# Where the FFN's moving operands lie in SBUF: one remainder of 512 bytes, or six

## The chip, the cores and the metric

One core of a Trainium2 chip runs the whole program. The metric is device time in microseconds, the median of several runs; before the change it is 2765.83 us, of three runs between 2764.89 and 2770.86.

## The reference

One decoder block on a sequence of 256 positions and 2048 channels in float32. A conditioning vector gives shifts, scales and gates. Two token mixers (Mamba-2 and Gated DeltaNet) run side by side on the normalised input and are merged. What the change touches is the dense FFN behind them:

```
x = x + gate_m * mix
h = modulate(rms_norm(x, norm_ffn_w), shift_f, scale_f)
gate, up = split(h @ w_gate_up)              # 2048 -> 2 x 5632
x = x + gate_f * ((silu(gate) * up) @ w_down) # 5632 -> 2048
return rms_norm(x, final_norm_w)
```

## The kernel before, in words

Activations lie transposed: a tile has 128 channels as partitions and, for each of KT = 16 (or FT = 44 in the FFN's hidden layer) groups of 128 channels, a row of S = 256 float32, one per position. A row is 1024 bytes, so all rows of a tile start at the same remainder modulo 512 bytes.

Every linear layer is a list of items. An item is one 512 KB block of weights: eight matrices of 128 x 128. `load_next` (L136) queues its DMA on SP, ACT copies it to `hi` with reduced precision (L146), DVE makes the rest `lo = raw - hi` (L148), and `lin_items` (L209) or `quad_items` (L230) issue three matmuls for each matrix:

```
T_.matmul(ps[:, t, :], hi[:, s], h_, ...)           # L221: stationary hi, moving high part
T_.matmul(ps[:, t, :], hi[:, s], al[:, kt, :], ...) # L222: stationary hi, moving low part
T_.matmul(ps[:, t, :], lo[:, s], h_, ...)           # L223: stationary lo, moving high part
```

The second argument is the stationary operand (the weights, 512 bytes per partition, at a multiple of 512), the third the moving operand (one row of the activation tile). So an item is 24 matmuls of 128x128 by 128x256, each with its weight load. `pump` (L155) issues one item at a time and keeps up to four prepared ahead; it also calls the posts, the work behind a finished accumulation. The order of the work on every engine is the order of these calls.

The FFN begins at L1252. A pool `ff` opens at the address where the mixer's pools were; a pad of OFF = 48 words comes first, so that the four tiles h2h, h2l (KT rows each, high and low part of h) and fh, fl (FT rows each, of the hidden layer) start 192 bytes past a multiple of 512. The mixer's moving operands (hh, hl, yh, yl, mh, ml) start at the same remainder in this program. L1266 to L1270 write the rows of h2h and h2l while the first items already run. The gate-up product is 24 items by `quad_items` (six accumulators side by side, so that four rows of h feed six items) and 152 by `lin_items`, in which the even items use rows 0 to 7 of h and the odd ones rows 8 to 15. `ffn_post` (L1222) writes row j of fh and fl. The down product is 88 items: for each of 8 pairs of output tiles, the 44 rows of fh and fl twice in order.

The z items (`z_items`, L255) have the operands the other way round: a row block of hh or hl is stationary and 512 columns of the weight tile, which start at a multiple of 512 bytes, are moving.

Of the kernel before, what the change touches and what calls it, by code (L numbers as in the profile page):

```python
# [10 lines left out]
F32 = mybir.dt.float32  # L11
F32R = mybir.dt.float32r
# [7 lines left out]
P = 128  # L20
D = 2048
S = 256
KT = D // P
# [3 lines left out]
FT = 44  # L27
# [23 lines left out]
NCA = 2  # L51
LZ = 2

OFF = 48

VB_ADA = 0
VN_MIX = 96
# [11 lines left out]
C_NSL = 2  # L69
C_LV = 6  # L70
C_I16 = C_LV * P + 3 * 64


@with_exitstack
def block_kernel(ctx: ExitStack, tc: tile.TileContext, xT, cvec, vec, dskip, consts,
# [44 lines left out]
    def vcol(i):  # L120
        return vs[:, i:i + 1]
# [33 lines left out]
    def pump():  # L155
        while items and len(ready) < LA + 1:
            load_next()
        while dots:
            dots.popleft()()
        did, old = False, len(posts)  # L160
        if ready and ready[0][2] <= st_["done"]:
            mm, post, need, sync, hi, lo = ready.popleft()
            if sync:
                finish_posts()
            old = len(posts)
            mm(hi, lo)
            posts.extend(post)
            st_["mm"] += 1
            did = True
        for _ in range(min(old, 1)):  # L170
            posts.popleft()()
        st_["wait"] -= 1.0
        if st_["gen"] is None and gens and gens[0][1] <= st_["mm"]:
            finish_posts()
            st_["gen"] = gens.popleft()
            st_["wait"] = 0.0
        if st_["gen"] is not None and (st_["wait"] <= 0.0 or not did):
            try:
                st_["wait"] = max(st_["wait"], -0.99) + next(st_["gen"][0]) * st_["gen"][2]
            except StopIteration:  # L180
                st_["gen"] = None
                st_["done"] += 1
        if old == 0 and len(posts) > 1:
            posts.popleft()()
        while len(posts) > PQ:
            posts.popleft()()
        st_["pumped"] += 1
        if side and st_["side"] and st_["pumped"] % st_["side"] == 0:
            side.popleft()()

    def flush():
        while items or ready or gens or st_["gen"] is not None:
            pump()
        finish_posts()
# [14 lines left out]
    def lin_items(blocks, xh, xl, nk, done, need=0, sync=False, late_need=0):  # L209
        hold = {}  # L210
        def mk(bi):
            def mm(hi, lo):
                ah, al = (xh(), xl()) if callable(xh) else (xh, xl)
                if bi == 0:
                    hold["ps"] = plin.tile([P, 2, S], F32, tag="lin", name="ps_lin")
                ps = hold["ps"]
                for j in range(BLK):
                    t, kt = divmod(bi * BLK + j, nk)
                    s = slice(j * P, (j + 1) * P)
                    h_ = ah[kt // 8][:, kt % 8, :] if isinstance(ah, list) else ah[:, kt, :]  # L220
                    T_.matmul(ps[:, t, :], hi[:, s], h_, start=kt == 0, stop=False)  # L221
                    T_.matmul(ps[:, t, :], hi[:, s], al[:, kt, :], start=False, stop=False)  # L222
                    T_.matmul(ps[:, t, :], lo[:, s], h_, start=False, stop=kt == nk - 1)  # L223
            return mm
        for bi, src in enumerate(blocks):
            last = bi == len(blocks) - 1
            post = [lambda f=f: f(hold["ps"]) for f in done] if last else []
            add_item(src, mk(bi), post, late_need if last and late_need else need, sync and bi == 0)
# [82 lines left out]
    def sq_finish():  # L311
        ps = bank("ps_sq", (P, S))
        for i, k in enumerate("ab"):
            for t in range(2):
                T_.matmul(ps, ones, sqa[k][:, t, :], start=i + t == 0, stop=i + t == 2)
        return ps

    def rstd_T(pool, ps):
        r = pool.tile([P, S], F32, tag="rstd", name="rstd")
        A.activation(r, ps, AF.Sqrt, scale=1.0 / D, bias=EPS)  # L320
        V.reciprocal(r, r)
        return r
# [18 lines left out]
    def finish_side():  # L341
        while side:
            side.popleft()()
        while dots:
            dots.popleft()()

    def ada_fin(j0, j1):
        V.tensor_tensor(ada[:, j0:j1], ada2[:, j0:j1, 0], ada2[:, j0:j1, 1], ADD)
        V.tensor_tensor(ada[:, j0:j1], ada[:, j0:j1], vs[:, VB_ADA + j0:VB_ADA + j1], ADD)
# [7 lines left out]
    with tc.tile_pool(name="st", bufs=1) as st:  # L357
# [97 lines left out]
        r = rstd_T(st, ps)  # L455
# [10 lines left out]
        for q in range(1, 4):  # L466
# [9 lines left out]
            if q == 2:  # L476
# [6 lines left out]
                lv = st.tile([P, 3, 64], F32, name="lv")  # L483
                nc.sync.dma_start(lv, consts[:, C_LV * P:C_I16].rearrange("p (a b) -> p a b", b=64))
                V.tensor_copy(lvm, lv)
# [230 lines left out]
    def gdn_mix(hu, units):  # L716
        unit = units[hu]
        nxt = units[hu + 1] if hu + 1 < NHU else None
        if hu == 0:
            pools["gp"] = gs.enter_context(tc.tile_pool(name="gp", bufs=1))  # L720
            pools["gsm"] = gs.enter_context(tc.tile_pool(name="gsm", bufs=2))
            pools["i16"] = pools["gp"].tile([64, 256], F32, name="i16")
            nc.sync.dma_start(pools["i16"], consts[0:64, C_I16:C_I16 + 256])
            seg_in, seg_out, squares, ssq, kq, scales, n_tile, store = gdn_head(hu, unit)
# [474 lines left out]
    def res_post(j, gate, pool):  # L1199
        def f(ps):  # L1200
            x2 = pools["accs"]
            for t in range(2):
                i = 2 * j + t
                V.scalar_tensor_tensor(x2[:, i, :], ps[:, t, :], gate[:, i:i + 1], x2[:, i, :], MUL, ADD)
            sq = pool.tile([P, 2, S], F32, tag="th" if j else "cacc", name="sq", bufs=1 if j or pool is not gl_ else NCA)
            A.activation(sq, x2[:, 2 * j:2 * j + 2, :], AF.Square)
            if j == 0:
                sqa["a"] = sq
            elif j < 7:
                G.tensor_tensor(sqa["a"], sqa["a"], sq, ADD)  # L1210
            else:
                sqa["b"] = sq
        return [f]
# [36 lines left out]
    phase_a.close()  # L1250

    with tc.tile_pool(name="ff", bufs=1) as ff:  # L1252
        ff.tile([P, OFF], F32, name="off")
        h2h = ff.tile([P, KT, S], F32R, name="h2h")
        h2l = ff.tile([P, KT, S], F32R, name="h2l")
        fh = ff.tile([P, FT, S], F32R, name="fh")
        fl = ff.tile([P, FT, S], F32R, name="fl")
        F_.update(h=h2h, l=h2l, fh=fh, fl=fl, ff=ff)
        tmps = {}
        for t in range(KT + 1):  # L1260
            if t in (5, 9, 13):
                for _ in range(6):
                    pump()
            if t < KT:
                tmps[t] = ff.tile([P, S], F32, tag="fth", name="htmp", bufs=2)
                V.scalar_tensor_tensor(tmps[t], x2[:, t, :], wsf[:, t:t + 1], rf, MUL, MUL)  # L1266
                A.activation(h2h[:, t, :], tmps[t], AF.Identity, bias=ada[:, 48 + t:49 + t])
            if t > 0:
                V.scalar_tensor_tensor(h2l[:, t - 1, :], tmps[t - 1], ada[:, 47 + t:48 + t],
                                       h2h[:, t - 1, :].bitcast(F32), ADD, SUB)  # L1270
        while items:
            pump()
        finish_side()
        gf = ff.tile([P, KT], F32, name="gf")
        for j in range(8):
            lin_items([w_dn[j, b] for b in range(11)], fh, fl, FT, res_post(j, gf, ff))
        ada_fin(80, 96)
        V.tensor_scalar(gf, ada[:, 80:96], 0.5, None, MUL)
        while len(items) > 20:
            pump()  # L1280
        for t in (1, 4, 7):
            A.activation(x2[:, t, :], x2[:, t, :], AF.Identity, scale=vcol(VN_FIN + t))
        A.activation(dum, ones[:, 0:1], AF.Sqrt)
        flush()
        r = rstd_T(ff, sq_finish())
        for t in range(KT):
            if t in (1, 4, 7):
                G.tensor_tensor(x2[:, t, :], x2[:, t, :], r, MUL)
            else:
                V.scalar_tensor_tensor(x2[:, t, :], x2[:, t, :], vcol(VN_FIN + t), r, MUL, MUL)  # L1290
            if t % 2 == 1:
                (nc.sync if t % 4 == 1 else nc.scalar).dma_start(out[:, t - 1:t + 1, :], x2[:, t - 1:t + 1, :])
# [101 lines left out]
```

## Time and profile before

| what | value |
|---|---|
| median of the runs | 2765.83 us |
| the profiled execution's own time | 2744.2 us |
| its span, first to last instruction | 2742.4 us |
| TensorE (PE) busy | 2665.7 us, 97% |
| VectorE (DVE) busy | 1884.0 us, 69% |
| ScalarE (ACT) busy | 1371.5 us, 50% |
| mean granted TensorE clock | 0.988 |
| FFN's first and last matmul | 1997.6 us, 2727.2 us |

Matmuls overlap: the duration that the profile gives for one is longer than the distance to the next one's start. What a row of matmuls costs is read from the starts, in the timeline. PEld is the weight load, which runs beside the matmul before it. A granted clock of 1.00 is 2.4 GHz, 0.50 is 1.2 GHz.

### The profile page before, as it was taken

Reading aid. Unit: us, or ns where it says so; the run is one execution under the profiler, and the core shown is the slowest. Engines: PE = TensorE matmul, PEld = TensorE weight load, DVE = VectorE, ACT = ScalarE, POOL = GpSimd, SP = SyncE. Lnnn points to the kernel's source line nnn. Section 1 sums busy time; section 2 is a strip of 40 time slices with the busy share of each in tenths; the row PEclk is TensorE's granted clock in tenths of the full one; section 3 lists DMA queues with packets and bytes.
Section 4 is the critical chain, followed back from the end, with each engine's and each line's share of the span. In section 5 each row is a group of like instructions: output and inputs, shape, how many; then the busy total and the mean of one; then the engine's idle time right before and its main releaser. Section 6 shows DMA issues by size and latency. Waiting matters only on the chain.

```text
span 2742.4 us, 51781 instructions
## 1 busy us (share of the span) xinstructions
PE 2665.7 (97%) x20930; PEld 2547.5 (93%) x20930; DVE 1884.0 (69%) x2794; ACT 1371.5 (50%) x2250; POOL 306.7 (11%) x684
## 2 busy tenths in 40 slices
PE   6999999999999999989999999999999999999998
PEld 5889899999999999988899989999989999999997
DVE  7787767769687786857767667768666666655444
ACT  3325554655546455544666656554444444444442
POOL 0000312303123131210000000002100000000000
PEclk8999999999999999999999999999999999999999
DMA  8886657566575665735545445447756666655553
GB/s 334 299 325 231 208 173 253 182 208 229 168 248 175 227 213 173 253 131 179 190 156 177 167 163 176 162 153 268 241 178 216 228 224 225 228 199 194 192 193 131
DMA packets 183283, 566.90 MB, mean 207 GB/s; under 512 B 34753, under 2 KB 43777, under 8 KB 183041
## 3 DMA queue, kind: packets, MB, share of 16 engines
q1 hardware_dynamic: 154306, 552.56, 59.0%
q10 hardware_dynamic: 28736, 11.01, 1.5%
q8 instruction: 164, 2.69, 0.4%
q14 instruction: 77, 0.63, 0.1%
HBM read 552.49 MB, written 11.01 MB: 205 GB/s over the span
## 4 chain that ended last, share of the span: by engine, by line
PE 64%; issue 21%; DVE 6%; DMA 4%; POOL 3%; ACT 2%; SPq 0%; ACTq 0%; DVEq 0%; POOLq 0%
PE ps_lin L221 14%; PE ps_lin L223 14%; PE ps_lin L222 14%; PE ps_z L268 2%; PE ps_z L270 2%; PE ps_z L269 2%; DMA araw<-in_w_ada 2%; DVE lo L148 2%; PE ps_lin L246 1%; PE tw L831 1%; PE td L839 1%; PE ps_q L406 1%; PE ps_lin L245 1%; PE ps_lin L247 1%; ACT hi L146 1%
## 5 line engine op out<-in xcount | busy, mean ns | idle before, releaser
L148 DVE TENSOR_TENSOR lo<-raw,hi 128x1024 fp32r<-128x1024 f32 x825 | 1012.3, 1232 | 673.4 <-ACT hi L146 670.6
L146 ACT CAST hi<-raw 128x1024 fp32r<-128x1024 f32 x825 | 860.5, 1049 | 527.1 <-PE ps_lin L222 259.5
L221 PE MATMUL ps_lin<-hh,hi 128*128 128x256 f32 x1792 | 510.1, 285 | 0.0
L222 PE MATMUL ps_lin<-hl,hi 128*128 128x256 f32 x1792 | 501.8, 280 | 0.0
L223 PE MATMUL ps_lin<-hh,lo 128*128 128x256 f32 x1792 | 501.7, 280 | 0.0
L222 PEld LDWEIGHTS ps_lin<-hl,hi 128*128 128x128 f32 x1792 | 340.3, 190 | 3.7 <-issue 2.4
L221 PEld LDWEIGHTS ps_lin<-hh,hi 128*128 128x128 f32 x1792 | 339.7, 190 | 4.1 <-issue 2.4
L223 PEld LDWEIGHTS ps_lin<-hh,lo 128*128 128x128 f32 x1792 | 340.7, 190 | 0.0
L223 PE MATMUL ps_lin<-h2h,lo 128*128 128x256 f32 x1216 | 335.7, 276 | 0.0
L222 PE MATMUL ps_lin<-h2l,hi 128*128 128x256 f32 x1216 | 335.6, 276 | 0.0
L221 PE MATMUL ps_lin<-h2h,hi 128*128 128x256 f32 x1216 | 335.6, 276 | 0.0
L221 PE MATMUL ps_lin<-yh,hi 128*128 128x256 f32 x896 | 255.0, 285 | 3.1 <-DVE accg L592 3.1
L222 PE MATMUL ps_lin<-yl,hi 128*128 128x256 f32 x896 | 250.0, 279 | 0.0
L223 PE MATMUL ps_lin<-yh,lo 128*128 128x256 f32 x896 | 249.9, 279 | 0.0
L223 PEld LDWEIGHTS ps_lin<-h2h,lo 128*128 128x128 f32 x1216 | 228.3, 188 | 0.2 <-DVE lo L148 0.2
L221 PEld LDWEIGHTS ps_lin<-h2h,hi 128*128 128x128 f32 x1216 | 228.3, 188 | 0.0
L222 PEld LDWEIGHTS ps_lin<-h2l,hi 128*128 128x128 f32 x1216 | 228.3, 188 | 0.0
L268 PE MATMUL ps_z<-hi,hh 128*128 128x512 f32 x512 | 206.8, 404 | 0.0
L270 PE MATMUL ps_z<-hi,hl 128*128 128x512 f32 x512 | 201.1, 393 | 0.0
L269 PE MATMUL ps_z<-lo,hh 128*128 128x512 f32 x512 | 200.6, 392 | 0.0
L223 PE MATMUL ps_lin<-fh,lo 128*128 128x256 f32 x704 | 194.3, 276 | 0.0
L221 PE MATMUL ps_lin<-fh,hi 128*128 128x256 f32 x704 | 194.3, 276 | 0.0
(328 smaller groups left out, 5416.6 us busy)
## 6 DMA issues: line engine op xcount, KB each, us to landing
raw<-in_w_gu SPq DMA_DIRECT2D x176, 512.0 KB, 4.2
raw<-in_w_g SPq DMA_DIRECT2D x143, 512.0 KB, 4.6
raw<-in_w_ada SPq DMA_DIRECT2D x128, 512.0 KB, 5.1
raw<-in_w_s SPq DMA_DIRECT2D x96, 512.0 KB, 4.1
raw<-in_w_dn SPq DMA_DIRECT2D x88, 512.0 KB, 4.3
araw<-in_w_ada SPq DMA_DIRECT2D x64, 512.0 KB, 7.8
raw<-in_w_gz SPq DMA_DIRECT2D x64, 512.0 KB, 4.5
raw<-in_w_gp SPq DMA_DIRECT2D x64, 512.0 KB, 3.9
```

The costliest lines, as they stand in the source:

```text
L146: A.copy(hi, raw)
L148: V.tensor_sub(lo, raw, hi.bitcast(F32))
L221: T_.matmul(ps[:, t, :], hi[:, s], h_, start=kt == 0, stop=False)
L222: T_.matmul(ps[:, t, :], hi[:, s], al[:, kt, :], start=False, stop=False)
L223: T_.matmul(ps[:, t, :], lo[:, s], h_, start=False, stop=kt == nk - 1)
L245: T_.matmul(ps[:, t, :], hi[:, s], h_, start=kt == 0 and t == 0, stop=False)
L246: T_.matmul(ps[:, t, :], hi[:, s], al[:, kt, :], start=False, stop=False)
L247: T_.matmul(ps[:, t, :], lo[:, s], h_, start=False, stop=kt == KT - 1 and t == 1)
L268: T_.matmul(pss[c], hh[:, kt, cs], hi[:, s], start=kt == 0, stop=False)
L269: T_.matmul(pss[c], hh[:, kt, cs], lo[:, s], start=False, stop=False)
L270: T_.matmul(pss[c], hl[:, kt, cs], hi[:, s], start=False, stop=kt == KT - 1)
L406: T_.matmul(ps[:, t, :], hi[:, s], x1[:, kt, :], start=first, stop=last)
```

## The change

In place of the pad and the four tiles the pool holds one tile `mov`. It is cut into six blocks, in the order of ROWS; before each block the position is raised to the next one with the block's remainder. A block of kind "h" holds 8 rows of the high part and then the same 8 rows of the low part of h; a block of kind "f" holds 11 rows of fh and then of fl. The class Rows lets the callers index rows as before.

```
-OFF = 48
+ROWS = [("f", 128), ("h", 256), ("h", 320), ("f", 352), ("f", 384), ("f", 416)]
+class Rows:
+    def __init__(self, tiles, n):
+        self.tiles, self.n = tiles, n
+
+    def __getitem__(self, ix):
+        p, r, c = ix
+        return self.tiles[r // self.n][p, r % self.n, c]
     with tc.tile_pool(name="ff", bufs=1) as ff:
-        ff.tile([P, OFF], F32, name="off")
-        h2h = ff.tile([P, KT, S], F32R, name="h2h")
-        h2l = ff.tile([P, KT, S], F32R, name="h2l")
-        fh = ff.tile([P, FT, S], F32R, name="fh")
-        fl = ff.tile([P, FT, S], F32R, name="fl")
+        groups = {"h": ([], []), "f": ([], [])}
+        words = sum(2 * S * (KT // 2 if k == "h" else FT // 4) for k, _ in ROWS) + ROWS[-1][1] // 4
+        big = ff.tile([P, words], F32R, name="mov")
+        pos = 0
+        for k, rem in ROWS:
+            pos += (rem // 4 - pos) % 128
+            n = KT // 2 if k == "h" else FT // 4
+            for part in groups[k]:
+                part.append(big[:, pos:pos + n * S].rearrange("p (a b) -> p a b", b=S))
+                pos += n * S
+        assert pos == words
+        h2h, h2l = (Rows(g, KT // 2) for g in groups["h"])
+        fh, fl = (Rows(g, FT // 4) for g in groups["f"])
```

So rows 0 to 7 of h are at 256 and rows 8 to 15 at 320; rows 0 to 10, 11 to 21, 22 to 32 and 33 to 43 of the hidden layer are at 128, 352, 384 and 416. Everything else in the program is the same.

## Rows read from the trace of the kernel before

**Rows 1.** The page: busy time, share of the span and instructions of each engine.

```profile
PE 2665.7 (97%) x20930; PEld 2547.5 (93%) x20930; DVE 1884.0 (69%) x2794; ACT 1371.5 (50%) x2250; POOL 306.7 (11%) x684
```

**Rows 2.** Stretches: length, busy us (count) of PE, PEld, DVE, ACT, POOL, clock, DMA share, GB/s.

```profile
2039.40:2042.60 3.20, 3.20 (x17) 3.20 (x17) 1.23 (x1) 1.39 (x2) 0.00 (x0) 0.50 0.13 44
2086.00:2486.00 400.00, 400.00 (x3532) 400.00 (x3531) 247.52 (x303) 176.03 (x222) 0.00 (x0) 1.00 0.66 223
2490.00:2726.00 236.00, 236.00 (x2085) 236.00 (x2084) 111.53 (x102) 95.09 (x97) 7.77 (x6) 1.00 0.53 179
```

**Rows 3.** Chain of waits, 2086 to 2727.5 us: start, length, what.

```profile
5661 pieces in order of time: start us, us, what
...
2085.97 0.12 PE ps_lin L223
...
2727.22 0.13 PE ps_lin L223
2727.37 0.48 DVE accs L1204
```

**Rows 4.** Timeline of PE, down product: start, duration (us); the first and last of 55 matmuls.

```profile
2499.82 0.28 PE L222 MATMUL ps_lin<-fl,hi 128*128 128x256 f32 x1
...
2505.94 0.28 PE L222 MATMUL ps_lin<-fl,hi 128*128 128x256 f32 x1
```

**Rows 5.** Groups of instructions, PE: line, tiles, shapes, count, busy us, mean ns.

```profile
L221 PE MATMUL ps_lin<-h2h,hi 128*128 128x256 f32 x1216 | 335.6, 276 | 0.0
...
L221 PE MATMUL ps_lin<-fh,hi 128*128 128x256 f32 x704 | 194.3, 276 | 0.0
...
L245 PE MATMUL ps_lin<-h2h,hi 128*128 128x256 f32 x192 | 54.8, 286 | 3.5 <-ACT h2h L1267 3.5
```

**Rows 6.** Timeline of PE at the half clock: the first and last of seven matmuls.

```profile
2039.72 0.41 PE L245 MATMUL ps_lin<-h2h,hi 128*128 128x256 f32 x1
...
2041.00 0.41 PE L245 MATMUL ps_lin<-h2h,hi 128*128 128x256 f32 x1
```

**Rows 7.** Timeline of PE, early FFN: the first and last of 54 matmuls.

```profile
2003.75 0.28 PE L245 MATMUL ps_lin<-h2h,hi 128*128 128x256 f32 x1
...
2009.99 0.28 PE L247 MATMUL ps_lin<-h2h,lo 128*128 128x256 f32 x1
```

**Rows 8.** Timeline of PE in the mixer: the first and last of 40 matmuls.

```profile
760.30 0.28 PE L223 MATMUL ps_lin<-hh,lo 128*128 128x256 f32 x1
...
764.89 0.28 PE L223 MATMUL ps_lin<-hh,lo 128*128 128x256 f32 x1
```

**Rows 9.** Timeline of PE, z matmuls in two places, 11 and 14 of them.

```profile
259.61 0.39 PE L270 MATMUL ps_z<-hi,hl 128*128 128x512 f32 x1
...
261.90 0.39 PE L268 MATMUL ps_z<-hi,hh 128*128 128x512 f32 x1
...
1336.79 0.40 PE L268 MATMUL ps_z<-hi,hh 128*128 128x512 f32 x1
...
1339.82 0.40 PE L269 MATMUL ps_z<-lo,hh 128*128 128x512 f32 x1
```

**Rows 10.** Timeline of PE behind the FFN's last wait: the first and last of six.

```profile
2085.57 0.28 PE L221 MATMUL ps_lin<-h2h,hi 128*128 128x256 f32 x1
...
2086.15 0.28 PE L223 MATMUL ps_lin<-h2h,lo 128*128 128x256 f32 x1
```

**Rows 11.** Instructions on tile h2h: duration ns min/median/max, first and last start.

```profile
L245 PE MATMUL ps_lin<-h2h,hi x192: 276/276/579, 1997.6 to 2073.8; 128*128 128x256 f32 x192
...
L1267 ACT ACTIVATE h2h<-htmp,ada x16: 496/508/510, 1997.0 to 2057.7; 128x256 fp32r<-128x256 f32 x16
```

**Rows 12.** Groups of instructions on DVE and ACT, 2097 to 2728 us.

```profile
L148 DVE TENSOR_TENSOR lo<-raw,hi 128x1024 fp32r<-128x1024 f32 x229 | 281.4, 1233 | 251.4 <-ACT hi L146 251.4
L146 ACT CAST hi<-raw 128x1024 fp32r<-128x1024 f32 x229 | 239.9, 1052 | 261.8 <-PE ps_lin L222 215.8 <-ACT hi L146 29.8 <-issue 14.2
```

## The prediction

> **What bounds the kernel now.** I read the page's first two parts, then the stretches of the FFN, then single instructions. TensorE is busy for 97% of the span [rows 1], and in the FFN it never rests: in the stretches 2086 to 2486 and 2490 to 2726 us PE is busy for the whole time at a granted clock of 1.00 (2.4 GHz), while DVE and ACT are busy for 62% and 44% of the first and less of the second [rows 2]. The chain of waits over the same time says it more sharply: from 2085.97 to 2727.22 us it holds 5660 matmuls, one after the other, and one DVE instruction after them; nothing else ends last [rows 3]. So the FFN's time is the number of its matmuls times the distance from one start to the next.
>
> That distance is (2727.22 - 2085.97) / 5659 = 113.3 ns, and the listing of single instructions has the same number for the down product alone: 54 steps from 2499.82 to 2505.94 us [rows 4]. The 276 ns that stand as a matmul's duration are not what it costs, since each overlaps the next two. The FFN has 3 x 1216 + 3 x 192 + 3 x 704 = 6336 such matmuls [rows 5], 718 us at that distance. Only what changes this distance can move the time by much.
>
> **Part 1: the address of the moving operand.** Each matmul streams a row of 256 float32 (1024 bytes) from h2h, h2l, fh or fl. Today every row starts 192 bytes past a multiple of 512; the weights that are loaded meanwhile start at a multiple of 512 (each of a tile's eight blocks is 512 bytes). After the change the h rows 0 to 7 start at 256 and 8 to 15 at 320, the f rows in groups of eleven at 128, 352, 384 and 416. The gate-up product's 4224 matmuls are shared equally by the two h groups, 2112 each; the down product's 2112 equally by the four f groups, 528 each. Number, shapes and order of the instructions stay.
>
> Does the distance depend on the remainder? The trace before has no stream of 256-column matmuls with another remainder, so I bound it by rows. Below: at the half clock (0.50, 1.2 GHz) the same matmuls stand 213.3 ns apart (2039.72 to 2041.00 us, 6 steps), which is 256 columns in 256 cycles with nothing lost [rows 2, 6]. At 2.4 GHz 256 cycles are 106.7 ns, so today's 113.3 holds 6.7 ns that are not streaming; no remainder can give back more: 6336 x 6.7 = 42 us.
>
> Above: the same operands at the same 192 bytes have a second, slower distance. From 2003.75 to 2009.99 us lie 53 steps of 117.7 ns, at full clock, with the same instructions [rows 7]; the stream keeps it until it is interrupted. A mixer stretch shows it as well: 39 steps from 760.30 to 764.89 us, 117.7 ns [rows 8]. So the stream has two steady paces, 113.3 and 117.7, and which one it takes is settled by how it is started after a wait. One more pair of rows bears on the remainder itself: the z matmuls, whose moving operand is a weight tile at remainder 0, take 229 ns for 512 columns (259.61 to 261.90 us, 10 steps) and in another place 233.1 (1336.79 to 1339.82, 13 steps) [rows 9]; per 256 columns that is 114.5 and 116.5, again two paces, 1.2 ns above and 1.2 below the two of remainder 192. Moving operand and weights have changed places there, so it is not a clean comparison, but it is the nearest that there is, and it says that remainder 0 and remainder 192 differ by about 1%, not by 5%. I take the low pace, 113.3 ns, as what every group keeps (change: nothing), with 106.7 and 117.7 as the ends of the range.
>
> The Trainium skill has a price for this distance in "TensorE: Matmul & The Clock Gate", section "Back-to-back issue gap": columns over 2.4 plus 2.5 ns, 109.2 ns for 256 columns, with no word of an address. The trace does not agree (113.3 at the full clock). If what is above the rule were a matter of placement, the rule's distance would be worth 6336 x 4.1 = 26 us; that is my estimate from that page, and the faster rival below stands without it.
>
> **Part 2: changing from group to group.** Steps between unequal remainders occur where none did: about 154 in the gate-up product (each of its later items uses the other half of the h rows) and 64 in the down product (8 pairs of output tiles, twice through four groups). What a disturbed stream costs until it is steady again is seen after the last wait, at 2085.57 us: the next five steps take 580 ns, some 13 over five times 113.3 [rows 10]. 218 such would be 2.9 us. Today the stream goes from h2h to h2l and from tile to tile without a trace of it, so I count nothing and keep the 3 us as an end.
>
> **Part 3: one tile in place of four.** All FFN rows become slices of the tile mov. If waits went by whole tiles, fh's writes would wait for reads of h. They go by rows already: the first matmul on h2h starts at 1997.6 us, while h2h is written until 2057.7 [rows 11]. The new tile is also first written when the four were: the first h2h row follows the sum of squares over all output tiles of w_o, so everything that used this memory is done. Cost nothing. The pad grows from 192 to 416 bytes and shifts only scratch tiles behind it.
>
> **Part 4: the other engines.** ACT and DVE write the rows and split the weights; the splitting takes them 1.05 and 1.23 us per item of 24 matmuls, for which PE takes 2.72 us [rows 12]. They have slack to hide a few ns whatever the address. If the matmuls went faster, an item at 24 x 106.7 = 2.56 us would still leave DVE, the busier of the two, under 70%.
>
> **Sum.** 2744.2 us for the profiled execution (span 2742.4) plus 0. The median of the runs, 2765.8, stands 21.6 us above that execution; I carry the change over to it: 2766 us.
>
> **Rivals.**
>
> *The slower pace (slower).* The FFN settles in the pace of 117.7 and, having no wait after 2085 us, keeps it to the end. Price (117.7 - 113.3) x 5660 = 25 us: 2791. For it: this pace exists at 192, and today's FFN ran in it for 15 us at its start before a wait ended it [rows 7]. A different remainder shifts the moving stream against the weight stream, which is what could turn the choice at the last restart. Against it: after that restart the stream fell back to 113.3 within five steps [rows 10]. It decides at that restart, or at any of the group steps.
>
> *Single groups are slower (slower).* Some remainders have only the slower pace or a still slower one. An h group at 117.7 costs 2112 x 4.4 = 9.3 us, an f group 528 x 4.4 = 2.3. One h group and one or two f groups: +12 to +14, about 2779. An f group alone would not be measurable. For it: the remainder 0 rows [rows 9]. Against it: nothing, but also no row that shows it.
>
> *Some groups are faster.* If both h groups gave back half of the 6.7 ns, 4224 x 3.3 = 14 us: 2752; all of it in all groups is 2724. For it: 6.7 ns is lost in each matmul, and not at the half clock [rows 6], so it is a matter of two streams meeting rather than of the array. Against it: the two paces of 192 and the two at 0 are all at or above 113.3, and no row at the full clock shows less for a one-cycle stream.
>
> *The change doesn't do what it says*, the tile being placed with other remainders: the pool starts where the 192 pad begins today, which is a multiple of 512, so I give this no chance of its own.
>
> **How the numbers follow.** About 0.2% (5.5 us) is what can be told from no change. Every group at 113.3, with up to 3 us for the group steps: 0.46, 2763 to 2770. Slower pace throughout: 0.17, 2791. Single groups slower: 0.17, 2772 to 2785. Faster groups: 0.20, 2724 to 2760. So faster 0.20, within 0.2% 0.46, slower 0.34. The predicted time is 2766. A range from 2748 to 2792 leaves out the larger half of the gains and little of the losses, under 2 in 10.
>
> **What would show it.** The start-to-start distance in four places: an item on h rows 0 to 7, the next on rows 8 to 15, and the f groups within one item stream of the down product. All at 113.3 proves part 1; a pace that alternates from item to item proves the single-group rival; 117.7 everywhere after the last restart proves the slower pace; anything below 113 proves the faster rival. The last row's end minus the start of the run of 5660 matmuls should be 641 us. Part 2 would show as single steps near 120 ns at the boundaries of groups, part 3 as a first h2h matmul or fh write that waits for something new. The mixer must keep its times up to 1991 us. The prediction is wrong if any group's distance differs from 113.3 by more than 1 ns.

## The result, and the profile after

The changed kernel takes 2780.45 us (median of 18 runs, 2773.8 to 2783.4) against 2765.36 for the kernel before (18 runs, 2744.6 to 2777.4). The ratio is 1.0062, with an interval of 1.0040 to 1.0085: slower by 0.6%, at the upper side of the predicted range. The profiled execution has a span of 2779.8 us against 2742.4, which is 37 us and not 15; why the two differ is one of the things that follow.

The page of the changed kernel (span; busy time and instructions, which answer to [rows 1]):

```profile
span 2779.8 us, 51781 instructions
...
PE 2698.7 (97%) x20930; PEld 2581.3 (93%) x20930; DVE 1883.4 (68%) x2794; ACT 1371.7 (49%) x2250; POOL 308.3 (11%) x684
```

TensorE does the same 20930 matmuls and is busy for 33.0 us more. DVE, ACT and POOL differ by under 2 us in sum; PEld goes with PE (33.8 us more).

Two stretches of the FFN in the changed kernel, with the columns of [rows 2]:

```profile
2086.00:2486.00 400.00, 400.00 (x3363) 400.00 (x3362) 237.76 (x290) 169.10 (x213) 0.00 (x0) 1.00 0.63 213
2490.00:2726.00 236.00, 236.00 (x1990) 236.00 (x1990) 111.37 (x108) 94.63 (x100) 6.49 (x5) 1.00 0.54 185
```

PE is as full and the clock as high as before, yet in 400 us it starts 3363 matmuls where it started 3532, and in the second stretch 1990 for 2085. So PE waits for nothing; each matmul takes longer to make room for the next.

The chain of waits in the changed kernel from 2086 us on (answers to [rows 3]):

```profile
5712 pieces in order of time: start us, us, what
...
2091.36 0.13 PE ps_lin L230
...
2764.58 0.13 PE ps_lin L232
2764.74 0.48 DVE accs L1213
```

Again the chain holds matmuls to its end and one DVE instruction; there are 5712 pieces and not 5661, since at 2086 us this kernel is some 50 matmuls further back. Among the longest is the first matmul of an item at 256, behind a step from 320, at 2091.36 us.

The timeline of PE in the gate-up product of the changed kernel; these three rows are the first matmuls of three items of 24, at remainders 320, 256 and 320:

```profile
2202.63 0.28 PE L230 MATMUL ps_lin<-mov,hi 128*128 128x256 f32 x1
...
2205.46 0.29 PE L230 MATMUL ps_lin<-mov,hi 128*128 128x256 f32 x1
...
2208.35 0.28 PE L230 MATMUL ps_lin<-mov,hi 128*128 128x256 f32 x1
```

The item at 320 takes 2.83 us, that at 256 takes 2.89: 117.9 and 120.4 ns for each matmul (120.1 as a mean over all items). At 113.3 either would take 2.72.

The timeline of PE in the down product, the first matmuls of the groups at 128, 352, 384, 416 and again 128, 33 matmuls each:

```profile
2513.98 0.28 PE L230 MATMUL ps_lin<-mov,hi 128*128 128x256 f32 x1
...
2517.90 0.28 PE L230 MATMUL ps_lin<-mov,hi 128*128 128x256 f32 x1
...
2521.86 0.28 PE L230 MATMUL ps_lin<-mov,hi 128*128 128x256 f32 x1
...
2525.77 0.28 PE L230 MATMUL ps_lin<-mov,hi 128*128 128x256 f32 x1
...
2529.64 0.28 PE L230 MATMUL ps_lin<-mov,hi 128*128 128x256 f32 x1
```

That is 118.8, 120.0, 118.5 and 117.3 ns. The account closes: 2112 x (120.1 - 113.3) + 2112 x (117.9 - 113.3) + 528 x (5.5 + 6.7 + 5.2 + 4.0) = 14.4 + 9.7 + 11.3 = 35.4 us, for an FFN that runs from its first matmul, at 2001.62 us,

```profile
2001.62 0.38 PE L254 MATMUL ps_lin<-mov,hi 128*128 128x256 f32 x1 [3.54 <-ACT mov L1284]
```

to 2764.58, 763.0 us; before it ran from 1997.6 [rows 11] to 2727.22, 729.6 us. The difference is 33.4 us; the first items partly wait or run at the half clock, where a step is no longer than before. In the changed kernel at the half clock, remainder 256 (the first and last of twelve matmuls):

```profile
2005.47 0.41 PE L254 MATMUL ps_lin<-mov,hi 128*128 128x256 f32 x1
...
2007.82 0.41 PE L256 MATMUL ps_lin<-mov,lo 128*128 128x256 f32 x1
```

11 steps of 213.6 ns, where [rows 6] have 213.3. The remaining 4.0 us of the 37 lie ahead of the FFN, in the mixer, where nothing was changed.

### The profile page after: what moved, and what is told of

Its sections match the earlier page's. It is cut to its first block, busy times and chain, and to the rows that moved or that the text cites. A ratio compares the mean times of both kernels' runs of the same rounds, so it can differ in the third digit from the quotient of the medians.

```text
span 2779.8 us, 51781 instructions
## 1 busy us (share of the span) xinstructions
PE 2698.7 (97%) x20930; PEld 2581.3 (93%) x20930; DVE 1883.4 (68%) x2794; ACT 1371.7 (49%) x2250; POOL 308.3 (11%) x684
## 4 chain that ended last, share of the span: by engine, by line
PE 75%; issue 13%; DVE 5%; DMA 3%; ACT 2%; POOL 2%; SPq 0%; DVEq 0%; ACTq 0%; POOLq 0%
PE ps_lin L230 17%; PE ps_lin L232 17%; PE ps_lin L231 17%; PE ps_z L277 3%; PE ps_z L279 3%; PE ps_z L278 3%; DMA araw<-in_w_ada 1%; DVE lo L157 1%; DVE araw L343 1%; PE ps_lin L255 1%; ACT hi L155 1%; PE td L848 1%; PE tw L840 1%; PE ps_lin L256 1%; PE ps_lin L254 1%
## 5 line engine op out<-in xcount | busy, mean ns | idle before, releaser
L230 PE MATMUL ps_lin<-mov,hi 128*128 128x256 f32 x1920 | 540.2, 281 | 0.0
L232 PE MATMUL ps_lin<-mov,lo 128*128 128x256 f32 x1920 | 540.0, 281 | 0.0
L231 PE MATMUL ps_lin<-mov,hi 128*128 128x256 f32 x1920 | 539.8, 281 | 0.0
L230 PEld LDWEIGHTS ps_lin<-mov,hi 128*128 128x128 f32 x1920 | 363.7, 189 | 0.0
L232 PEld LDWEIGHTS ps_lin<-mov,lo 128*128 128x128 f32 x1920 | 362.8, 189 | 0.0
L231 PEld LDWEIGHTS ps_lin<-mov,hi 128*128 128x128 f32 x1920 | 362.5, 189 | 0.0
L230 PEld LDWEIGHTS ps_lin<-yh,hi 128*128 128x128 f32 x896 | 168.9, 188 | 4.3 <-issue 1.9
L231 PEld LDWEIGHTS ps_lin<-yl,hi 128*128 128x128 f32 x896 | 169.0, 189 | 1.3
```

## The experiments

Each experiment's rows are two stretches inside the FFN, the first in the gate-up, the second in the down product: length, PE busy (count), granted clock, DMA share, GB/s. The distance is the length over the count less 2.4, since a window also counts the two or three matmuls that it cuts. For the kernel before, this gives 113.3 and 113.4 ns:

```profile
2100.00:2480.00 380.00, 380.00 (x3356) 1.00 0.66 221
2540.00:2720.00 180.00, 180.00 (x1590) 1.00 0.53 182
```

In e6, e9, e11 and e12 the scratch row of the last normalisation also shares a buffer, to make room. From the start of the last FFN matmul to the end these four traces take 15.35 to 15.37 us, the kernel before 15.36, so this edit costs nothing that is seen.

**e1.** Four tiles as before; the pads differ, and fh and fl lie ahead of h2h and h2l (the comments are not in the kernel). Does a remainder keep its pace where no group steps occur?

```
-        ff.tile([P, OFF], F32, name="off")
+        ff.tile([P, F_REM // 4], F32, name="off")               # fh, fl at 128
...
+        ff.tile([P, (H_REM - F_REM) // 4], F32, name="off2")    # h2h, h2l at 256
```

> The four separate tiles of before, but all rows of h at remainder 256 and all rows of fh and fl at 128, so no remainder changes within a product. Theory (each remainder has its own pace against the weight stream): the gate-up product's matmuls stand 120.0 ns apart from first to last, the down product's 118.5, and the run takes about 2782 us. Rival (the change from group to group costs the time): both products run at 113.3 or at 117.8, 2745 or 2770 us. Rival (the one tile with high and low parts nearer to each other costs it): also 113.3 or 117.8.

```profile
2100.00:2480.00 380.00, 380.00 (x3169) 1.00 0.65 210
2540.00:2720.00 180.00, 180.00 (x1519) 1.00 0.59 185
```

120.0 and 118.7 ns; the run took 2779.9 us. No step, no common tile, and the paces of the changed kernel are there. Both rivals fall.

**e2.** Such pads for h at 320 and f at 352, with the tiles in the order of before.

> The four separate tiles, all rows of h at remainder 320, all rows of fh and fl at 352. Theory (own pace for each remainder): 117.8 ns in the gate-up product and about 120 in the down product, some 2776 us. Rivals (group steps; one tile): 113.3 or 117.8 in both, 2745 or 2770 us.

```profile
2100.00:2480.00 380.00, 380.00 (x3229) 1.00 0.67 214
2540.00:2720.00 180.00, 180.00 (x1503) 1.00 0.58 184
```

117.8 and 120.0 ns; 2780.1 us. An early stretch of the h rows in this run, between two waits, went otherwise (timeline of PE, the first and last of 55 matmuls):

```profile
2026.80 0.28 PE L247 MATMUL ps_lin<-h2h,lo 128*128 128x256 f32 x1
...
2032.92 0.28 PE L247 MATMUL ps_lin<-h2h,lo 128*128 128x256 f32 x1
```

That is 113.3 ns for a step. So 320 has two paces, 113.3 and 117.8, like 192 before [rows 3, 7].

**e3.** h at 416, f at 384, in the order of e1.

> The four separate tiles, all rows of h at remainder 416, all rows of fh and fl at 384. Theory (own pace for each remainder): about 117.5 ns in the gate-up product and about 118.8 in the down product, some 2773 us. Rivals (group steps; one tile): 113.3 or 117.8 in both, 2745 or 2770 us.

```profile
2100.00:2480.00 380.00, 380.00 (x3241) 1.00 0.67 216
2540.00:2720.00 180.00, 180.00 (x1520) 1.00 0.58 185
```

117.3 and 118.6 ns; 2776.2 us. As expected from the groups of the changed kernel.

**e4.** The changed kernel with every group at 192.

```
-ROWS = [("f", 128), ("h", 256), ("h", 320), ("f", 352), ("f", 384), ("f", 416)]
+ROWS = [("f", 192), ("h", 192), ("h", 192), ("f", 192), ("f", 192), ("f", 192)]
```

> The changed kernel with its one tile and its six groups, but each group at remainder 192. Theory (own pace for each remainder): the two paces of before, 113.3 or 117.8 ns for a whole run, so single times in two clusters near 2747 and near 2770 us, as the kernel before. Rival (the one tile, with the high and low parts nearer to each other, costs the time): 117.8 to 120 in every run, about 2780 us. Rival (group steps): as the kernel before, since no remainder changes.

```profile
2100.00:2480.00 380.00, 380.00 (x3229) 1.00 0.67 214
2540.00:2720.00 180.00, 180.00 (x1531) 1.00 0.59 187
```

Ten runs: four from 2744.3 to 2752.4 us and six from 2771.2 to 2775.3, nothing between; ratio to before 0.9985 (0.9941 to 1.0030). The one tile has no cost that this interval would show. The profile is one of the slower ones (2774.1 us) and stands at 117.8 ns in both products. So the kernel before has two times as well: with 5660 matmuls behind the last wait, 113.3 or 117.8 is 25 us. Its 18 runs beside the changed kernel are seven from 2744.6 to 2749.1 and eleven from 2761.1 to 2777.4. Its profiled execution, 2744.2 us, is none of the 18 and lies beside the seven. That the slower eleven stood at 117.8 is inferred from this twin, since no other run of the kernel before was profiled.

**e5, e6, e7.** The edit of e2 with other remainders, to see whether 192 is special.

> The four separate tiles, h at remainder 0, fh and fl at 64. Theory (each remainder has its own paces, set by where the moving stream stands against the weight stream): steady paces in each product that differ from 113.3, since 0 lets both streams begin on the same remainder; I expect 117 to 122 ns in both and 2770 to 2795 us. Rival (only the remainders of the change are slow, 192 is nothing special): 113.3 or 117.8 in both.

```profile
2100.00:2480.00 380.00, 380.00 (x3169) 1.00 0.65 210
2540.00:2720.00 180.00, 180.00 (x1531) 1.00 0.60 187
```

120.0 at 0 and 117.8 at 64; 2779.6 us.

> The four separate tiles, h at remainder 288, fh and fl at 448 (the scratch row of the last normalisation shares a buffer, to make room). Theory (own paces for each remainder): a multiple of 64 that is odd, 448 = 7 x 64 like 192 and 320, has the fast pace 113.3 among its paces; 288, which is no multiple of 64, has not, and runs at 117 to 120 ns. Rival (no order in the remainders): anything from 113 to 122 in both.

```profile
2100.00:2480.00 380.00, 380.00 (x3260) 1.00 0.67 216
2540.00:2720.00 180.00, 180.00 (x1591) 1.00 0.62 194
```

116.7 at 288 and 113.3 at 448; 2761.5 us. The guess about odd multiples of 64 held for 448; 64 itself stood at 117.8 in e5.

> The four separate tiles, h at remainder 160, fh and fl at 224, the two neighbours of 192 at 32 bytes. Theory (own paces for each remainder, 113.3 only at odd multiples of 64): both stand at 116 to 120 ns, 2765 to 2785 us. Rival (the pace changes gradually with the remainder): between 113.3 and 120, nearer to 192's paces than 128 and 256 are, so below 118 in both.

```profile
2100.00:2480.00 380.00, 380.00 (x3205) 1.00 0.66 213
2540.00:2720.00 180.00, 180.00 (x1523) 1.00 0.58 185
```

118.7 at 160 and 118.3 at 224; 2778.7 us. The pace does not change gradually: 32 bytes to either side of 192 the distance is above both that 192 has, 5 ns above the lower and under 1 ns above the higher.

**e8.** Is it the moving operand's address, or its distance from the weights'? 64 bytes ahead of the weight tiles move them to remainder 64, and the mixer's operands to 256.

```
-OFF = 48
+OFF = 32
...
+    wp.tile([P, 16], F32, tag="wpad", name="wpad", bufs=1)
```

> The kernel before with 64 bytes put ahead of the weight tiles, which moves the weights to remainder 64 and the mixer's operands to 256, and a pad of 32 words in the FFN, so that its rows stay at 192. Theory (what counts is the moving operand's remainder less the weights'): the mixer, at a difference of 192, keeps 113.3 and 117.8 ns; the FFN, at 128, stands at 118.7 as remainder 128 did. Rival (the moving operand's own remainder counts): the mixer stands at 120.0 as remainder 256 did, the FFN at 113.3 or 117.8.

The first row is a stretch of the mixer's last product (moving operand at 256), the others are the FFN (moving operand at 192):

```profile
1925.00:1975.00 50.00, 50.00 (x444) 1.00 0.73 249
2100.00:2480.00 380.00, 380.00 (x3204) 1.00 0.66 212
2540.00:2720.00 180.00, 180.00 (x1520) 1.00 0.58 186
```

The mixer runs at 50 / (444 - 2.4), 113.2 ns, at the very remainder where e1's FFN took 120.0, and over the whole mixer 48 of its stretches of 30 or more matmuls end at 113.3 and 32 at 117.8, as in the other traces. The FFN at 192 runs at 118.7, the pace of remainder 128 in e1. What counts is the difference, 192 in the one and 128 in the other. This is the run that decides: the pace depends on where the moving operand stands against the weight tiles. That it is the load of the next weights that the moving stream meets is the nearest reading, but an inference.

**e9.** All rows of the FFN at 448, which e6 had shown at 113.3 only.

> The four separate tiles, all rows of the FFN at remainder 448 (the last normalisation's scratch row shares a buffer, to make room). Theory (odd multiples of 64 have the two paces 113.3 and 117.8, and which one holds is settled by the start after the last wait): times in two clusters, near 2747 and near 2772 us, as the kernel before. Rival (448 has only the fast pace): every run near 2747 us, 1% under the median of the kernel before.

```profile
2100.00:2480.00 380.00, 380.00 (x3229) 1.00 0.66 213
2540.00:2720.00 180.00, 180.00 (x1530) 1.00 0.59 187
```

117.8 in the profile; ten runs, four from 2740.6 to 2749.9 us and six from 2768.3 to 2780.1. Two clusters again, so 448 is like 192 and no better.

**e10.** Items that step between 192 and 320.

```
+ROWS = [("f", 192), ("h", 192), ("h", 320), ("f", 320), ("f", 320), ("f", 320)]
```

> The changed kernel's one tile, with rows 0 to 7 of h at 192 and 8 to 15 at 320, rows 0 to 10 of fh and fl at 192 and the others at 320. All four have the paces 113.3 and 117.8, but the stream now goes from one remainder to another after each item. Theory (a group step moves the two streams against each other and can settle the pace anew): the pace changes at some of the steps, so that single times no longer fall into two clusters and lie between 2750 and 2770 us. Rival (a steady pace, once taken, is kept across the steps): two clusters, near 2747 and 2772 us.

The first matmuls of three items of 24, at 192, 320 and 192:

```profile
2200.28 0.28 PE L230 MATMUL ps_lin<-mov,hi 128*128 128x256 f32 x1
...
2203.01 0.28 PE L230 MATMUL ps_lin<-mov,hi 128*128 128x256 f32 x1
...
2205.83 0.28 PE L230 MATMUL ps_lin<-mov,hi 128*128 128x256 f32 x1
```

The item at 192 takes 2.73 us (113.8 ns), the one at 320 takes 2.82 (117.5), and so it goes in all later gate-up items of this trace, and in the down product's groups (113.5 at 192, 117.8 at 320). A step does settle the pace anew. The ten runs spread from 2758.9 to 2771.6 us without two clusters, median 2763.8; ratio 1.0005 (0.9968 to 1.0043).

**e11.** Rows 0 to 7 of h at 288, all others at 448.

```
+ROWS = [("h", 288), ("h", 448), ("f", 448), ("f", 448), ("f", 448), ("f", 448)]
```

> One tile, rows 0 to 7 of h at 288, rows 8 to 15 and all of fh and fl at 448. In the kernel with h at 288 and f at 448 the step from 288 to 448 led into the fast pace. Theory (a step from a remainder with one pace enters the next always in the same way): 116.7 ns in the items at 288, 113.3 in those at 448 and in the down product, in every run; 2742 + 2112 x 3.3 ns + some 20 us between profile and median times at worst, so one cluster at about 2755 us, under the median of the kernel before. Rival (the pace behind a step is left to chance): times spread from 2752 to 2775 us.

The first matmuls of three items, at 288, 448 and 288:

```profile
2201.82 0.28 PE L230 MATMUL ps_lin<-mov,hi 128*128 128x256 f32 x1
...
2204.62 0.28 PE L230 MATMUL ps_lin<-mov,hi 128*128 128x256 f32 x1
...
2207.36 0.28 PE L230 MATMUL ps_lin<-mov,hi 128*128 128x256 f32 x1
```

2.80 us at 288 and 2.74 at 448; the down product stands at 113.3. Ten runs from 2751.3 to 2762.9 us, median 2754.6: one cluster, ratio to before 0.9955 (0.9926 to 0.9984) in a batch in which 6 of 25 runs of the kernel before were under 2755 us. Its slowest run, 2762.9, is below the fastest of the changed kernel, 2773.8.

**e12.** Only odd multiples of 64, with the steps that had looked harmless.

```
+ROWS = [("f", 3, 64), ("h", 0, 192), ("f", 2, 192), ("f", 1, 320), ("f", 0, 448), ("h", 1, 448)]
```

> One tile, odd multiples of 64 only: rows 0 to 7 of h at 192 and 8 to 15 at 448, so that each step between the halves is 256 bytes; the four groups of fh and fl at 448, 320, 192 and 64 in the order in which they are used, so that each step goes 128 bytes back. Theory (the pace behind a step is set by the step: forward by 64 or 128 bytes it became 117.8, forward by 160 and back by 128 it became 113.3): 113.3 ns everywhere but for some 7 ns at each of about 220 steps, in every run; one cluster near 2747 us, 0.9% under the kernel before. Rival (it depends on the pace ahead of the step or on the remainder, not on the step alone): 117.8 in part of the groups, 2752 to 2775 us.

The first row lies ahead of the last wait of the FFN, the others behind it:

```profile
2060.00:2083.00 23.00, 23.00 (x205) 1.00 0.52 163
2100.00:2480.00 380.00, 380.00 (x3229) 1.00 0.66 213
2540.00:2720.00 180.00, 180.00 (x1530) 1.00 0.58 186
```

113.5, then 117.8 and 117.8. Across steps of 256 bytes whichever pace held went on, ahead of the wait the low one (over four such steps) and behind it the high one; and steps of 128 back, which led to 113.3 in e10, did nothing here. The theory that the step alone sets the pace falls. Twelve runs, seven from 2746.9 to 2752.9 us, one at 2760.2 and four from 2767.0 to 2771.3; ratio 1.0013 (0.9980 to 1.0047). In this batch 12 of 17 runs of the kernel before were under 2755 us, median 2748.4, below e11's 2754.6. So whether e11 beats the kernel before depends on how often that one takes its low pace: over all batches in 28 of 74 runs, but from 3 of 13 in e4's batch to 12 of 17 in this one. The 0.6% of the result is such a mix too: against the median of 2748.4 in this batch the changed kernel's 2780.45 would stand 1.2% higher, an estimate across batches.

## Why the prediction was right or wrong

*Right: what bounds the FFN, and the size of the term.* The FFN's time was the count times the distance, and no engine or wait took part. Of the two ends the upper was too low: 117.7 came from remainder 192, and 256 and 352 have 120.0.

*Wrong: the choice in part 1.* "I take the low pace, 113.3 ns, as what every group keeps" is the step that failed; all six groups stand at 117.3 to 120.1. By the prediction's own sign, a group more than 1 ns from 113.3, it was wrong. What happened is the rival of slower single groups, with all groups and not two. It had been given 0.17, with the words that no row shows it, and none did. The working leaned on [rows 9] instead, which it read as "remainder 0 and remainder 192 differ by about 1%, not by 5%". That reading failed: at remainder 0 the distance is 120.0 (e5), 5.9% above 113.3. In [rows 9] the moving operand is at 0 but the stationary one at 192, so by e8 the difference that counts there is 320, and at 320 the matmuls of 256 columns have the same two paces as at 192 (e2).

*Wrong: what stands between the profile and the median.* The 21.6 us were carried over as if they lay outside the program. The profiled execution had the low pace (2744.2 us) and most runs, as e4 suggests, the high one; the two paces of [rows 3] and [rows 7] were seen, and their price over the FFN, 25 us, was even worked out, but as a rival for the changed kernel and not as what the runs before already do. From the profile the change costs 35 us, a mean distance of 113.3 + 35.4 / 6336 = 118.9 ns. From the high pace it costs 6336 x (118.9 - 117.8) = 7 us; the changed kernel's median is 9.6 over that of the eleven slower runs, 2770.9, and what makes up the other 2.6 is open. The medians of all runs, 15 apart, lie between the two.

*Right in the main: parts 2 to 4.* e4 has the new tile and the groups, and its ratio to before is 0.9985. Group steps cost little: the mean of the items at 256 is 120.1 where the steady pace is 120.0 (e1). That a step can change the pace was priced as a transient and is more than that (e10, e11); it did not show here because 256 has one pace only and the step from it to 320 always led to 117.8.

*Right by chance: the total.* The working had a change of 0 where the profiled executions differ by 37 us, 35 of them by the pace; and its base, the median, stood 21.6 us above the profiled execution, most likely since most runs had the high pace already. The two errors of opposite sign left 2766 against 2780, 0.5% apart. The prediction's 109.2 ns from the Trainium skill ("TensorE: Matmul & The Clock Gate", section "Back-to-back issue gap") was not reached in any run: the least distance measured is 113.3. The section itself calls that formula the gap of an isolated matmul, which the prediction left out.

What stays open: why 192, 320 and 448 have the low pace (64, the other odd multiple of 64, was seen at 117.8 alone, in e5 and e12), and what settles it at a start. In the fourteen traces of this study 1144 stretches of 30 or more matmuls with remainders 192 apart (ps_lin in mixer and FFN, no step of 130 ns or more inside) end so, by the last 20 steps: 685 at 113.3, 458 at 117.8, and none at another distance but for one that breaks off with a step of 124. Why a step from 320 to 192 led to 113.3 in e10 and not in e12 was not found either. Whether the next weights' load or its own restart is what the stream meets could not be tried by taking the load away, since each matmul here brings its own.

## What to carry to other kernels

Where TensorE is full and matmuls of 256 float32 columns alternate with weight loads, read the distance between starts, not durations, and compare it for each operand: a shift of 32 bytes in where a tile starts was worth up to 5% of it (113.3 against 118.7). Choose the moving operand's start by its distance from the weights modulo 512, and expect more than one steady pace at the same addresses. Before carrying a profile's span over to a median, see whether the single times fall into clusters, and which one the profile belongs to.

## What the runs showed of the hardware

Distance between starts at 2.4 GHz, matmuls of 128x128 by 128x256 with a weight load each, by the moving operand's remainder less the weights' (modulo 512 bytes: the weight matrices of an item lie 512 bytes apart, the rows 1024, and the steady pace is the same for all of them):

| difference | steady distances seen, ns |
|---|---|
| 0, 256, 352 | 120.0 |
| 128, 384 | 118.7 |
| 160 | 118.7, in one early stretch 120.0 |
| 224 | 118.3 |
| 288 | 116.7, in some stretches 117.8 |
| 416 | 117.3, in some stretches 118.7 |
| 64 | 117.8 |
| 192, 320, 448 | 113.3 or 117.8 |

The paces are sharp: the means over each 240 matmuls of a steady stretch agree within 0.02 ns, whatever ACT, DVE and the DMAs do beside it. The single steps repeat in a short round: at 128 they go 122, 120, 119, 115, 117 ns over and over (e1, down product), at 352 121, 116, 125, 116, 123, 119 (e2); at 113.3, and at the 120.0 of 0 and 256, all steps are alike within the nanosecond that the trace resolves. At 1.2 GHz the distance was 213 ns at 192 and at 256. The Trainium skill says in "SBUF — State Buffer", section "Who interferes with whom", that PE never waits on another user of the SBUF; with that these sharp paces agree. It also says, in "TensorE: Matmul & The Clock Gate", section "What happens when you issue a matmul", that loading the next weights takes no read bandwidth from the running matmul; e8 speaks against it, since moving the weights by 64 bytes changed the FFN's distance from 113.3 or 117.8 to 118.7 ns with the moving operand at the same remainder. That it is the load itself that does it is not shown.
